# Chunk recurrence: the part of y that needs no u stacked into the u0 product, the rest accumulated in eight products of one shape

## The chip, the cores and the metric

The kernel runs on one core of one Trainium2 chip. The metric is device time in microseconds, the median of several runs. The engines of a core are TensorE (PE in the rows; its weight loads stand apart as PEld), VectorE (DVE), ScalarE (ACT), GpSimd (POOL) and SyncE (SP, which here issues most transfers). Each takes its instructions in a fixed order and waits at one until what that one needs is there.

## The reference

One layer of a hybrid encoder, 1024 tokens by 1024 columns in float32: an input projection, three token mixers side by side, an output projection with a residual, and a SwiGLU feed-forward part with a residual. The mixers are RWKV-7 time mixing (8 heads of 64), latent attention (4 heads) and stick-breaking attention (4 heads). The change is in the first. Its core is a recurrence over tokens, for each head with a 64x64 state S:

```
sa = S a_t
S  = S * w_t + sa b_t^T + v_t k_t^T
y_t = S r_t
```

After it, y is normed over each head, gets a bonus term, is multiplied by a gate and goes into the output projection.

## The kernel before, in words

The tokens are cut into 16 chunks of 64 (`NCH`, `L`). Inside a chunk the recurrence is solved by matrix products; only the state S goes from chunk to chunk. An early stage (`s1`, `s2`, `s3`) makes for each chunk and head the scaled vectors a and r (tile `AR`: a in the first 64 columns, r in the last), b and k (tile `BK`), and their masked products `gs` = (b|k) x (a|r), and writes them to the scratch tensor `d_ch` in DRAM. `d_lt` and `d_rx` are two parts of it. Another stage writes the inverse of I - A to the lower 64 rows of `d_rx`.

The recurrence itself is `chain_step(c)` (lines 1114 to 1155), called for the 16 chunks in turn. `chain_loads` brings 1 MB of `d_ch` into tile `CT` (its parts: `Lt`, `BKt`, `RX`) and v into the lower half of tile `SU`; both tiles have two buffers, and the transfers are issued from ACT's queue. `SU[:, 0]` is S stacked over v, `SU[:, 1]` is u stacked over v. Each step has four groups of products, eight heads each:

- u0 (L1124): `Lt[:, h, 0:64]` with S over v, 128 rows and 64 columns of weights. ACT copies the result (L1126, tile `u0s`).
- u (L1135): the inverse in `RX[64:128]` with u0, 64 rows and 64 columns. ACT copies it into `SU` (L1136).
- s (L1141): `BKt` with u over v, 128 x 64; DVE adds the decayed old state (tile `PS`) and writes the next S.
- y: for each head two products into the same place, one of `Lt[:, h, 64:128]` with u over v (L1148, 128 x 64) and one of `RX[0:64]` with S (L1149, 64 x 64).

A product in float32 is carried out as two instructions, so that eight products are 16 instructions in the rows. y of two chunks fills the upper and lower half of one bank of PSUM, and every second step `group_rows` copies it to SBUF and squares it (L1163 and L1165, ACT), and DVE sums the squares (L1168). After chunks 7 and 15 `rw_finish` norms and gates eight chunks at a time.

PSUM has eight banks in this stage: five under tag `b` for other work, one `av`, one `cu` (u0, u and s in turn) and one `cy` (y).

Between the groups `fill(us)` takes pieces of a background stream: first the last projections, then the two attentions, stick-breaking heads first (products z at L953 and L954, transposes wt at L890, products av at L908 to L915; scans C at L961 on DVE), latent heads after (products m at L976 to L978). A scheduler then sets each engine's order from the program's order and its own estimate; nothing moves on the chip after that. When the 16 steps are over, what is left of the stream runs by itself, and the output projection follows.

Of the kernel before, what the change touches and what calls it, by code (L numbers as in the profile page):

```python
# [20 lines left out]
P = 128  # L21
# [37 lines left out]
def trunk_kernel(ctx: ExitStack, tc: tile.TileContext, a: dict, out: bass.AP):  # L59
# [33 lines left out]
    # ---------------------------------------------------------------- constants  # L93
# [10 lines left out]
    # rotary tables  # L104
# [11 lines left out]
    # ---------------------------------------------------------------- DRAM scratch  # L116
# [19 lines left out]
    # ---------------------------------------------------------------- row norm and transpose  # L136
# [3 lines left out]
    def norm_transpose(pool, xt, dsts, tb):  # L140
        """rows of xt -> rms norm * gB -> transposed, split into dsts[h|l][group]"""
# [30 lines left out]
    # ---------------------------------------------------------------- streamed weights  # L172
# [27 lines left out]
    # xT[half][0 = h, 1 = l][group of 4 d blocks]  # L200
# [14 lines left out]
    def inproj_cols(c0, name):  # L215
        """w_in[:, c0:c0+128] as [c, t], one bank for each half of t"""
        if name in begun:
            return begun.pop(name)
        w = in_weights(c0, name)
        return [in_half(w, hf, name) for hf in range(2)]  # L220

    with tc.tile_pool(name="p0", bufs=2, reuse_waits="tile") as p0:
# [26 lines left out]
        for tb in range(NT):  # L249
# [3 lines left out]
            # the first projections, a quarter of t at a time  # L253
# [6 lines left out]
    # small constants of the attentions  # L260
# [11 lines left out]
    def shifted(dst, os_, cb):  # L272
        """dst[hf] = (1 - mu) p + mu p one step earlier"""
# [19 lines left out]
    # k_rope and the stick-breaking v, by row  # L293
# [25 lines left out]
    def sb_half(dst, blk, nm, hf, o):  # L319
        """[c, t] of two heads -> high and low parts, by head"""  # L320
# [11 lines left out]
    # ---------------------------------------------------------------- RWKV: projections, chunk products  # L332
    with tc.tile_pool(name="qa", bufs=1) as qa:
# [6 lines left out]
        # mask of the chunk products: rows (b|k) x s, columns (a|r) x t  # L340
# [14 lines left out]
        # up-projections of the two low ranks: K = 128 of (h, l) or (l, h), against the same rows twice  # L355
# [52 lines left out]
        def sigmoid3(dst, o, bias, t_):  # L408
            """dst = sigmoid(o - bias) = exp(-ln(1 + exp(bias - o)))"""
# [4 lines left out]
        def s1(pr, hf):  # L414
# [4 lines left out]
            # log decay / -kappa = sigmoid(w0 + u); its running sum in each chunk  # L419
# [16 lines left out]
        def s2(pr, hf):  # L436
# [20 lines left out]
            for e in range(2):  # L457
                cs_, rows_ = slice(hf * 8, hf * 8 + 8), slice(e * 64, e * 64 + 64)
                nc.sync.dma_start(d_lt[cs_, 0:64, 2 * pr + e, 0:64].rearrange("c k t -> k c t"), AR[rows_, :, 0, :])
                nc.sync.dma_start(d_rx[cs_, 0:64, 2 * pr + e, :].rearrange("c k t -> k c t"), AR[rows_, :, 1, :])  # L460
            tmp[n] = (AR, BK, av)

        def s3(pr, hf):
# [3 lines left out]
            # products of each chunk  # L467
            for q in range(2):
                c0 = hf * 8 + q * 4
                for e in range(2):  # L470
# [8 lines left out]
                    nc.sync.dma_start(d_lt[c0 : c0 + 4, 0:64, 2 * pr + e, 64:128].rearrange("c s t -> s c t"), gs[0:64, :, 64:128])  # L479
                    nc.sync.dma_start(d_a[2 * pr + e, c0 : c0 + 4].rearrange("c s t -> s c t"), gs[0:64, :, 0:64])  # L480
            # b, k times the decay of the whole chunk, transposed
            BKv = BK.rearrange("p c a t -> p c (a t)")
            tt(nc.vector, BKv, BKv, plt[:, pr, hf * 8 : hf * 8 + 8][:, :, None].to_broadcast([P, 8, 2 * L]), ALU.mult)
            # values, each head less its mean, by row
# [6 lines left out]
            # bonus * v  # L491
# [61 lines left out]
    # ---------------------------------------------------------------- two streams of work: the recurrence, and what fills its waits  # L553
# [4 lines left out]
    def fill(us):  # L558
        """trace about this much tensor-engine time of the background stream"""
# [29 lines left out]
    # ---------------------------------------------------------------- inverse of I - A_ab in every chunk; the other projections  # L589
# [28 lines left out]
    def inverse_steps(j0, j1):  # L618
        """back substitution of both diagonal blocks: XB[b] = (I - A_bb)^-T, one row for each step; GpSimd keeps the rows
        that are needed last up to date"""  # L620
# [24 lines left out]
    # four heads side by side on the partitions  # L645
# [10 lines left out]
    def merge_a(h):  # L656
        """(A_21 X_11) for the 16 chunks of a head, rows of the second half on partitions"""
# [14 lines left out]
    # MLA weights  # L672
# [936 lines left out]
```

## Time and profile before

| | |
|---|---|
| median of 3 runs | 1508.38 us |
| the three runs | 1508.38, 1509.59, 1500.39 us |
| span of the profiled execution, first to last instruction | 1507.6 us |
| its own time as a run | not given apart from the span |
| PE busy in the span | 1431.6 us (95%) |
| DVE busy | 918.1 us (61%) |
| ACT busy | 651.1 us (43%) |
| first u0 product to last y product | 434.6 to 723.7 us |

Only a span is known of the profiled execution, so sums are made against 1507.6 us; the median of the runs lies 0.8 us above it. A row of a product names weights as rows*columns and then the moving operand, as in `128*64 128x64`. PE's rows overlap: products are pipelined, and the time that a group takes on PE is best read from its start to the start of the next group. [...]

### The profile page before, as it was taken

The page shows a single profiled execution, that of the slowest core. Times are in us where ns is not written, and L with a number is a line of the kernel's source. Part 1 is how long each engine was busy: PE and PEld are TensorE (multiplying, and loading weights), DVE is VectorE, ACT ScalarE, POOL GpSimd, SP SyncE. Part 2 cuts the span into 40 slices and gives each one's busy share as a digit, 9 for nine tenths or more (in the row PEclk, how much of TensorE's full clock was granted, in tenths as well). Part 3 has the DMA queues.
Part 4 walks back from the last instruction along what each step waited for, and adds up shares of the span by engine and source line. Part 5 has one row for each costly group of instructions (what it writes and reads, how often), then busy time and mean ns, then how long its engine had stood idle before and what let it go on. Part 6 is the DMA issues. An engine that isn't in the chain of part 4 may idle for free.

```text
span 1507.6 us, 21884 instructions
## 1 busy us (share of the span) xinstructions
PE 1431.6 (95%) x7973; PEld 1164.0 (77%) x7973; DVE 918.1 (61%) x1308; ACT 651.1 (43%) x1256; POOL 639.4 (42%) x617
## 2 busy tenths in 40 slices
PE   7899999987979997999999899999999999999998
PEld 7677778876867876788788678888888888878786
DVE  5675566293336779654615885555555554798756
ACT  5745434223436656665723533233332332434342
POOL 1321111383233233212431676666665564645443
PEclk9999999998869998998999999999999999999999
DMA  7244656846558632542254153222222214953331
GB/s 210 64 112 117 153 122 164 178 113 155 144 167 247 187 116 88 153 135 85 92 174 160 39 186 105 98 93 90 88 100 101 102 50 183 379 175 114 98 133 70
DMA packets 222788, 201.31 MB, mean 134 GB/s; under 512 B 83373, under 2 KB 171738, under 8 KB 220762
## 3 DMA queue, kind: packets, MB, share of 16 engines
q1 hardware_dynamic: 212010, 175.28, 38.9%
q10 hardware_dynamic: 10672, 24.64, 5.0%
q8 instruction: 63, 1.03, 0.3%
q14 instruction: 43, 0.35, 0.1%
HBM read 131.95 MB, written 67.93 MB: 133 GB/s over the span
## 4 chain that ended last, share of the span: by engine, by line
PE 80%; DVE 11%; DMA 4%; ACT 2%; issue 2%; SPq 1%; POOL 0%; DVEq 0%; ACTq 0%; POOLq 0%
PE fd L197 4%; PE fd L198 4%; PE fd L196 4%; PE y L1149 2%; PE y L1148 2%; PE wt L890 2%; PE wo L198 2%; PE wo L197 2%; PE wo L196 2%; DVE XB L91 1%; PE u L1124 1%; PE s L1141 1%; PE u L1135 1%; PE ip_v L196 1%; DVE TM L91 1%
## 5 line engine op out<-in xcount | busy, mean ns | idle before, releaser
L91 POOL TENSOR_TENSOR l_h<-hr,h_h 128x512 fp32r<-128x512 f32 x77 | 106.9, 1389 | 105.5 <-ACT h_h L1270 101.7
L197 PE MATMUL fd<-l_w,h_h 128*128 128x512 f32 x308 | 119.7, 393 | 7.3 <-DVE l_w L91 7.3
L198 PE MATMUL fd<-h_w,l_h 128*128 128x512 f32 x308 | 118.5, 390 | 0.0
L91 DVE TENSOR_TENSOR l_w<-wd,h_w 128x512 fp32r<-128x512 f32 x77 | 89.7, 1174 | 47.0 <-ACT h_w L1270 47.0
L1270 ACT ACTIVATE h_h<-hr 128x512 fp32r<-128x512 f32 x77 | 48.7, 632 | 133.5 <-PE fd L197 89.2
L196 PE MATMUL fd<-h_w,h_h 128*128 128x512 f32 x308 | 83.6, 390 | 0.0
L91 POOL TENSOR_TENSOR l_ffn_w_up<-rffn_w_up,h_ffn_w_up 128x512 fp32r<-128x512 f32 x33 | 44.6, 1351 | 72.7 <-ACT h_ffn_w_up L1270 72.7
L197 PEld LDWEIGHTS fd<-l_w,h_h 128*128 128x128 f32 x308 | 57.8, 188 | 22.4 <-DVE l_w L91 10.6
L91 DVE TENSOR_TENSOR wtl<-wt,wth 128x512 fp32r<-128x512 f32 (+2 forms) x112 | 54.0, 492 | 34.5 <-PE av L914 12.0
L196 PEld LDWEIGHTS fd<-h_w,h_h 128*128 128x128 f32 x308 | 57.9, 188 | 12.1
L198 PEld LDWEIGHTS fd<-h_w,l_h 128*128 128x128 f32 x308 | 57.9, 188 | 11.8
L91 POOL TENSOR_TENSOR hid<-hid,up 128x512 f32<-128x512 f32 x44 | 62.7, 1425 | 9.6 <-DVE up L91 9.6
L91 POOL TENSOR_TENSOR l_ffn_w_gate<-rffn_w_gate,h_ffn_w_gate 128x512 fp32r<-128x512 f32 x33 | 47.5, 1442 | 28.0 <-ACT h_ffn_w_gate L1270 28.0
L895 ACT ACTIVATE wth<-wt 128x512 fp32r<-128x512 f32 (+2 forms) x112 | 48.9, 446 | 23.1 <-PE wt L890 10.7
L1449 ACT ACTIVATE hid<-hid 128x512 f32<-128x512 f32 x44 | 27.8, 634 | 57.2 <-DVE hid L91 57.2
L196 PE MATMUL wo<-woh,mix 128*128 128x512 f32 x128 | 50.5, 397 | 0.0
L198 PE MATMUL wo<-woh,mix 128*128 128x512 f32 x128 | 50.2, 394 | 0.0
L197 PE MATMUL wo<-wol,mix 128*128 128x512 f32 x128 | 50.1, 394 | 0.0
L1270 ACT ACTIVATE h_w<-wd 128x512 fp32r<-128x512 f32 x77 | 47.6, 618 | 0.9 <-PE fd L198 0.4
L1270 ACT ACTIVATE h_ffn_w_gate<-rffn_w_gate 128x512 fp32r<-128x512 f32 x33 | 20.7, 630 | 57.9 <-PE P4up L197 22.3
L1149 PE MATMUL y<-SU,CT 64*64 64x64 f32 x256 | 43.8, 254 | 0.0
L1148 PE MATMUL y<-SU,CT 128*64 128x64 f32 x256 | 43.4, 253 | 0.0
(565 smaller groups left out, 4503.9 us busy)
## 6 DMA issues: line engine op xcount, KB each, us to landing
CT<-d_ch ACTq DMA_DIRECT2D x15, 1024.0 KB
hr<-d_h SPq DMA_DIRECT2D x14, 1024.0 KB
rffn_w_gate<-in_ffn_w_gate_dram SPq DMA_DIRECT2D x11, 1024.0 KB
rffn_w_up<-in_ffn_w_up_dram SPq DMA_DIRECT2D x11, 1024.0 KB
d_h<-up SPq DMA_DIRECT2D x44, 256.0 KB
d_h<-hid SPq DMA_DIRECT2D x33, 256.0 KB
wd<-in_ffn_w_down_dram SPq DMA_DIRECT2D x8, 1024.0 KB
hr<-d_h SPq DMA_DIRECT2D x7, 768.0 KB
```

What stands on the lines that cost most here:

```text
L91: eng.tensor_tensor(o, x, y, op=op)
L196: nc.tensor.matmul(o, lh, rh, start=first, stop=False)
L197: nc.tensor.matmul(o, lh, rl, start=False, stop=False)
L198: nc.tensor.matmul(o, ll, rh, start=False, stop=last)
L890: nc.tensor.transpose(o[:, (sb * 2 + i) * P : (sb * 2 + i + 1) * P], W[i][:, (2 * g + sb) * P : (2 * g + sb + 1) * P], ident)
L895: nc.scalar.activation(wh[:, lo:hi], o[:, lo:hi], AF.Copy)
L1124: nc.tensor.matmul(o[0:64, hs[h]], Lt[:, h, 0:64], S[:, hs[h]], start=True, stop=True)
L1135: nc.tensor.matmul(o[0:64, hs[h]], RX[64:128, h, :], u0[:, hs[h]], start=True, stop=True)
L1148: nc.tensor.matmul(y[r0 : r0 + 64, hs[h]], Lt[:, h, 64:128], U[:, hs[h]], start=True, stop=False)
L1149: nc.tensor.matmul(y[r0 : r0 + 64, hs[h]], RX[0:64, h, :], S[0:64, hs[h]], start=False, stop=True)
L1270: nc.scalar.activation(hv, src, AF.Copy)
L1449: nc.scalar.activation(hid[f][hf], hid[f][hf], AF.Silu)
```

## The change

y is taken apart in another way. For each head, the r-part of `AR` and the (k,r)-products of `gs` now stand in the right 64 columns of `Lt`, below each other, so that one product of all 128 columns of `Lt` with S over v gives u0 in the upper 64 rows of a bank and the part of y that needs no u in the lower 64. `RX[0:64]` now holds the (b,r)-products, and eight products of it with u (64 x 64) are added onto that lower half. The bank is of tag `cy`, a new one for each chunk; u and s stay in `cu`. `y_rows` replaces `group_rows`: it copies y out after each step, 64 rows at a time, and squares and sums every second step, now from the copy in SBUF. In `s2` two transfers of halves of `AR` become one of the whole; in `s3` one transfer goes to `d_rx` instead of `d_lt`. The rest of the diff takes out comments.

```diff
@@ s2
-                nc.sync.dma_start(d_lt[cs_, 0:64, 2 * pr + e, 0:64].rearrange("c k t -> k c t"), AR[rows_, :, 0, :])
-                nc.sync.dma_start(d_rx[cs_, 0:64, 2 * pr + e, :].rearrange("c k t -> k c t"), AR[rows_, :, 1, :])
+                nc.sync.dma_start(d_lt[cs_, 0:64, 2 * pr + e, :].rearrange("c k t -> k c t"),
+                                  AR[rows_].rearrange("p c a t -> p c (a t)"))
@@ s3
-                    nc.sync.dma_start(d_lt[c0 : c0 + 4, 0:64, 2 * pr + e, 64:128].rearrange("c s t -> s c t"), gs[0:64, :, 64:128])
+                    nc.sync.dma_start(d_rx[c0 : c0 + 4, 0:64, 2 * pr + e, :].rearrange("c s t -> s c t"), gs[0:64, :, 64:128])
@@ chain_step
-        o = bank(f"u0_{c}", "cu")
+        yo = bank(f"y_{c}", "cy")
         for h in range(RWH):
-            nc.tensor.matmul(o[0:64, hs[h]], Lt[:, h, 0:64], S[:, hs[h]], start=True, stop=True)
+            nc.tensor.matmul(yo[:, hs[h]], Lt[:, h, :], S[:, hs[h]], start=h == 0, stop=True, skip_group_check=True)
         u0 = qr.tile([P, RWW], F32, tag="u0", bufs=1, name=f"u0s{c}")[64:128]
-        nc.scalar.activation(u0, o[0:64, :], AF.Copy)
+        nc.scalar.activation(u0, yo[0:64, :], AF.Copy)
...
-        if c % 2 == 0:
-            state["y"] = bank(f"y_{c}", "cy")
-        y = state["y"]
-        r0 = (c % 2) * 64
         for h in range(RWH):
-            nc.tensor.matmul(y[r0 : r0 + 64, hs[h]], Lt[:, h, 64:128], U[:, hs[h]], start=True, stop=False)
-            nc.tensor.matmul(y[r0 : r0 + 64, hs[h]], RX[0:64, h, :], S[0:64, hs[h]], start=False, stop=True)
+            nc.tensor.matmul(yo[64:128, hs[h]], RX[0:64, h, :], U[0:64, hs[h]], start=False, stop=True, skip_group_check=True)
         state["n"] = nxt
-        if c % 2 == 1:
-            group_rows(c // 2, y)
-            if c % 8 == 7:
-                side.append(rw_finish(c // 8, list(yn4), gnv["v"]))
+        y_rows(c, yo[64:128, :])
+        if c % 8 == 7:
+            side.append(rw_finish(c // 8, list(yn4), gnv["v"]))
         fill(FILL)
...
-    def group_rows(tb, y):
-        while side:
+    def y_rows(c, y):
+        while side and c % 2 == 0:
             fill(0.1)
-        yn = qr.tile([P, RWW], F32, tag="yn", bufs=4, name=f"yn{tb}")
-        nc.scalar.activation(yn, y, AF.Copy)
+        tb = c // 2
+        if c % 2 == 0:
+            yn4[tb % 4] = qr.tile([P, RWW], F32, tag="yn", bufs=4, name=f"yn{tb}")
+        yn = yn4[tb % 4]
+        nc.scalar.activation(yn[c % 2 * 64 : c % 2 * 64 + 64], y, AF.Copy)
+        if c % 2 == 0:
+            return
         sq = qr.tile([P, HALF], F32, tag="gq", bufs=1, name=f"gnq{tb}")
-        nc.scalar.activation(sq, y, AF.Square)
+        nc.scalar.activation(sq, yn, AF.Square)
...
-        yn4[tb % 4] = yn
```

The order on PE around the end of chunk 14, before (a row is one product here; s is the state, y the two kinds in turn, av and wt are background work, u_15 is u0 of the last chunk):

```order
L1141 MATMUL s_7021<-SU_6706,CT_6705 64x64 x8
L1148 MATMUL y_7031<-SU_6706,CT_6705 64x64
L1149 MATMUL y_7031<-SU_6706,CT_6705 64x64
L1148 MATMUL y_7031<-SU_6706,CT_6705 64x64
L1149 MATMUL y_7031<-SU_6706,CT_6705 64x64
...
L908 MATMUL av_1_7077<-wth_11_7015,vt_6790 128x256
...
L915 MATMUL av_1_7077<-wtl_10_7054,vt_6790 128x256
L1124 MATMUL u_15_7089<-SU_6908,CT_6907 64x64 x8
L890 MATMUL wt_22_7122<-ident,mw_4_6992 128x128
```

and the same place in the changed kernel (y_6768 is y of chunk 14, y_6954 the bank of chunk 15):

```order
L1142 MATMUL s_6893<-SU_6587,CT_6586 64x64 x8
L1145 MATMUL y_6768<-SU_6587,CT_6586 64x64 x8
L976 MATMUL m_4_512_6974<-mqk_6665,mqk_6663 128x128
...
L908 MATMUL av_1_6942<-wth_11_6887,vt_6671 128x256
...
L915 MATMUL av_1_6942<-wtl_10_6919,vt_6671 128x256
L890 MATMUL wt_22_6987<-ident,mw_4_6864 128x128
L1125 MATMUL y_6954<-SU_6780,CT_6779 128x64 x8
L890 MATMUL wt_21_6997<-ident,mw_4_6864 128x128
```

Where 16 products of two shapes stood in turn, eight of one shape stand; the u0 products write 128 rows, and other work stands between y and the next u0 as before. Over the whole recurrence PE's list changes the shape of its weights (rows*columns) 377 times before and 98 times now; whole blocks alone, with other work only between them, would make 335 and 78 of these. The one place where nothing stands between y and the next u0 is the end of chunk 1:

```order
L956 MATMUL z_2_0_4180<-sb_mask,identb 128x128
L1142 MATMUL s_4385<-SU_4080,CT_4079 64x64 x8
L1145 MATMUL y_4247<-SU_4080,CT_4079 64x64 x8
L1125 MATMUL y_4465<-SU_4259,CT_4258 128x64 x8
L890 MATMUL wt_00_4191<-ident,w_0_4137 128x128
```

There the u0 products moved up to y's end. Of the other steps the shortest distance is seven products.

On ACT, the order from the copy of y of chunk 3 to the copy of u0 of chunk 4, in the changed kernel (SU and CT are the next loads, yt a load for `rw_finish`, st, w and wth background work):

```order
L1162 ACTIVATE yn_4596<-y_4640 64x512
L1107 DMA SU_4867<-d_v 64x2x512
L1109 DMA CT_4866<-d_ch 128x2048
L957 ACTIVATE st_0_4507<-z_0_0_4511 128x128
L895 ACTIVATE wth_33_4523<-wt_33_4519 128x256
L1166 ACTIVATE gnq_4809<-yn_4596 128x512
...
L895 ACTIVATE wth_33_4523<-wt_33_4519 128x128
L1127 ACTIVATE u0s_4864<-y_4855 64x512
```

The copy of y stands ahead of the loads here as it did before, but now in every step instead of every second, and with 64 rows.

## Rows read from the trace of the kernel before

**Rows 1.** The page: busy time and share of each engine; who ends last, by engine.
```profile
PE 1431.6 (95%) x7973; PEld 1164.0 (77%) x7973; DVE 918.1 (61%) x1308; ACT 651.1 (43%) x1256; POOL 639.4 (42%) x617
...
PE 80%; DVE 11%; DMA 4%; ACT 2%; issue 2%; SPq 1%; POOL 0%; DVEq 0%; ACTq 0%; POOLq 0%
```

**Rows 2.** Chain of waits, 434 to 725 us: its shares by line.
```profile
by line: PE y L1149 12.0%; PE y L1148 11.3%; PE wt L890 10.7%; PE u L1124 7.1%; PE s L1141 5.6%; PE u L1135 5.5%; PE av L915 4.2%; PE z L953 3.7%; PE av L914 3.7%; DMA d_mk<-tqk 3.7%; PE m L976 3.2%; PE z L954 2.8%; PE m L977 2.6%; DVE C L9
```

**Rows 3.** Windows: length, busy us (instructions) per engine, granted clock, DMA share, GB/s.
```profile
434.00:460.00 26.00, 23.45 (x135) 19.13 (x136) 7.29 (x12) 8.44 (x16) 8.29 (x18) 0.58 0.71 234
460.00:570.00 110.00, 110.00 (x897) 87.73 (x895) 81.92 (x130) 68.92 (x163) 31.80 (x53) 0.92 0.60 177
570.00:620.00 50.00, 41.29 (x257) 33.91 (x256) 44.83 (x96) 31.75 (x78) 19.92 (x21) 0.86 0.24 75
620.00:725.00 105.00, 103.53 (x863) 86.41 (x862) 52.77 (x148) 59.66 (x153) 21.13 (x22) 0.90 0.40 122
```

**Rows 4.** Timeline of PE around a y block: start, us, line, tile, shape.
```profile
675.93 1.15 PE L1141 MATMUL s<-SU,CT 128*64 128x64 f32 x16
676.91 0.28 PE L1148 MATMUL y<-SU,CT 128*64 128x64 f32 x2
677.12 0.33 PE L1149 MATMUL y<-SU,CT 64*64 64x64 f32 x2
677.38 0.33 PE L1148 MATMUL y<-SU,CT 128*64 128x64 f32 x2
...
680.97 0.58 PE L915 MATMUL av<-wtl,vt 128*128 128x256 f32 x1
```

**Rows 5.** Timeline of PE: u block at 474 us and u0 block at 640 us, with what follows.
```profile
474.22 1.14 PE L1135 MATMUL u<-u0s,CT 64*64 64x64 f32 x16
475.30 0.50 PE L953 MATMUL z<-sqk,sqk 128*128 128x512 f32 x1
...
639.87 1.20 PE L1124 MATMUL u<-SU,CT 128*64 128x64 f32 x16
640.99 0.33 PE L890 MATMUL wt<-ident,mw 128*128 128x128 f32 x1
```

**Rows 6.** Timeline of PE: blocks whose weights have 128 columns, with what follows.
```profile
89.42 2.82 PE L474 MATMUL g<-AR,BK 64*128 64x128 f32 x32
92.17 1.16 PE L487 MATMUL vt<-cent,V 128*128 128x128 f32 x8
93.17 1.02 PE L493 MATMUL bo<-av,onesblk 128*128 128x512 f32 x2
...
398.81 0.95 PE L711 MATMUL lrkv<-bias_n,ctsckv 128*128 128x1 f32 x8
399.62 0.48 PE L196 MATMUL ukv<-ukvh,ct0ckv 128*128 128x512 f32 x1
```

**Rows 7.** Timeline of PE: half of the first y block, at the low clock.
```profile
444.01 0.42 PE L1148 MATMUL y<-SU,CT 128*64 128x64 f32 x2
444.36 0.47 PE L1149 MATMUL y<-SU,CT 64*64 64x64 f32 x2
...
447.19 1.94 PE L742 MATMUL tqk<-ident,Kt 128*96 128x128 f32 x8
```

**Rows 8.** Windows of PE alone: length, busy (instructions), granted clock, DMA share, GB/s.
```profile
632.00:634.00 2.00, 2.00 (x22) 1.00 0.20 74
634.00:636.00 2.00, 2.00 (x18) 1.00 0.00 0
636.00:638.00 2.00, 2.00 (x11) 0.65 0.15 40
638.00:640.00 2.00, 2.00 (x9) 0.50 0.86 292
640.00:642.00 2.00, 2.00 (x25) 1.00 0.98 373
...
588.00:590.00 2.00, 0.68 (x3) 0.50 0.32 82
```

**Rows 9.** Copies of u0 (L1126) and y (L1163) on ACT: ns, starts; what L1163 waited for.
```profile
L1126 ACT ACTIVATE u0s<-u x16: 588/589/592, 437.8 to 713.2; 64x512 f32<-64x512 f32 x16
...
L1163 ACT ACTIVATE yn<-y x8: 597/597/598, 469.4 to 723.9; 128x512 f32<-128x512 f32 x8
...
  PE y L1149: 18.0, 7
```

**Rows 10.** Weight loads and products of u (L1135): ns min/median/max, first and last start.
```profile
L1135 PEld LDWEIGHTS u<-u0s,CT x256: 129/135/224, 438.5 to 716.4; 64*64 64x64 f32 x128
L1135 PE MATMUL u<-u0s,CT x256: 217/218/364, 438.5 to 716.5; 64*64 64x64 f32 x128
```

**Rows 11.** Waits of PE in 434 to 725 us: total, times, longest.
```profile
PE u L1124 <- DMA CT<-d_ch: 6.1, 1, 6.1
...
PE u L1135 <- ACT u0s L1126: 1.9, 1, 1.9
```

**Rows 12.** Transfers of AR on SP's queue: ns of an issue.
```profile
L460 SPq DMA_DIRECT2D d_ch<-AR x16: 580/607/697, 65.7 to 245.4; - x16
```

## Prediction, made before the changed kernel was run

> **What bounds the kernel now.** I read the page first. PE is busy 95% of the span and ends 80% of the chain of waits [rows 1], so work taken off PE is the first thing that can shorten the run; DVE, with 61%, is the next. The change touches the stretch from 434 to 725 us. There the chain by line [rows 2] puts the two y lines on top: 12.0% and 11.3% of 291 us, 68 us. Next to them stand the background transposes; the DVE and DMA lines are small. The windows [rows 3] split the stretch in four. In the second (stick-breaking heads, y of chunks 1 to 7) PE has no gap in 110 us and DVE is at 74%. In the third (y of chunk 8 only) DVE is at 90% and PE at 83%: there PE waits for DVE. In the fourth (latent heads, chunks 9 to 15) PE is at 99%, DVE at 50%, ACT at 57%. PE's own list of waits names hardly anything [rows 11].
>
> The timeline shows why y is dear. At 676.91 us [rows 4] its 32 instructions run to 680.97 us: 4.06 us. Each pair of one shape starts 0.255 us after the pair of the other. The u block, 16 instructions of one shape, takes 1.08 us, 0.0675 each [rows 5]; a pair at that pace is 0.135 us, so a change of shape costs 0.12 us. y pays it 15 times in a block.
>
> **The change, part by part** (per block at the full clock, times 16).
>
> The y products. 32 instructions of two shapes become 16 of 64*64, the shape and count of the u block: 4.06 - 1.08 = 2.98 us less, 47.7 us in all. [...] Between s (128*64) and the new y there is a change of shape that was not there before: 16 x 0.12 = 1.9 us more.
>
> [...] The u blocks [rows 10] show loads of 135 ns and products of 218 ns, which in turn would need 353 ns per instruction; in the block one starts every 67.5 ns, on one group of rows and with float32 weights. [...]
>
> The u0 products. The weights go from 128 to all 128 columns of 128 rows; before, the block took 1.12 us [rows 5]. No row has 128*128 weights in float32 with 64 moving columns. Bounds [rows 6]: `g` (64*128, 128 moving columns) takes 2.75 us for 32, 1.4 for 16; `lrkv` (128*128, one column) 0.81 for 8, 1.6 for 16; `vt` (128*128, 128 columns) 1.00 for 8, 2.0 for 16. I take 1.8, between the two with the same weights: 0.68 x 16 = 10.9 us more, ends 4 and 14. On the other side u0 now has the shape of the background around it, so that one change of shape at its start goes: -1.9.
>
> Blocks cut by other work. The lists on PE hold 42 changes of shape beyond whole blocks before and 20 after, 22 x 0.12 = 2.6 us less.
>
> The clock. [...] A pass through 2 us windows puts it behind y blocks: the one at 632 to 636 us leaves 0.65 and 0.50 with PE busy all the time [rows 8]. [...]
>
> Sum on PE: -47.7 - 1.5 + 1.9 + 10.9 - 1.9 - 2.6 - 9 = -50 us.
>
> What does not reach the end. In the second stretch seven sixteenths of the terms without the clock (41 us), plus 4 of the clock's 9, are 22 us: PE would do it in 88 us, with DVE's 81.9 us in it at 93%. The highest share DVE has where it sets the pace is 90% [rows 3], 91 us, and there PE has gaps; I take 95 us, 7 us given back. The third stretch is DVE's already: its one block, 2.6 us, is given back whole. In the first stretch PE waits 6.1 us for the loads [rows 11] and other work goes on at the low clock: 1 us back. In the fourth, 23 us less would leave ACT at 73% and DVE at 64%: 2 us back. Together 12.6.
>
> ACT copies y 16 times instead of 8. A copy takes 0.6 us with 128 rows and with 64 [rows 9], so 4.8 us more. ACT has 40% of its time free, and it lost 18.0 us waiting for y's end in seven of the eight copies [rows 9], a wait that gets shorter with the block: 0, ends -4 and +5. The square now reads SBUF: nothing. DVE and POOL get nothing new. DMA: 32 transfers of `AR` become 16; at 0.6 us of issue on SP's queue [rows 12] that is 10 us less queue in 200 us, hidden behind PE: 0, ends -3 and 0. The loads of `CT` stand on ACT behind y's copy as before and leave earlier, with the block.
>
> Sum: -50 + 12.6 = -37.4 us. Against the span of 1507.6 us that is 1470.2; the median stands 0.8 us above the span, so **1471 us**. With the ends of u0 (-7, +3), the clock (-10, +9), what is given back (-6, +8) this case runs from 1450 to 1490.
>
> **The rivals.**
>
> *DVE keeps the second half.* PE's gain in the stick-breaking heads turns into waits for DVE, and the gaps bring the clock down as at 588 us, where 0.68 us busy of 2.00 goes with 0.50 [rows 8]. For it: DVE at 74% and then 90% [rows 3]. Against it: part of DVE's idle time there is waiting for PE. Then only the fourth stretch pays, some 18 us, and the first 3: 1487 us, 1480 to 1498. 14%.
>
> *The one bank for y (slower).* u0 of the next chunk needs the bank that ACT must first empty. ACT takes its work in order; if the copy stands behind background work, PE, in order too, stands still with all that is queued behind u0: background, u, s. The rows price one such pass through ACT in the open at 1.9 us [rows 11]. The gain is used up from 37/15 = 2.5 us per step; at two passes, 3.8 us, the loss is 57 - 37 = 20 us: 1528. For it: at the end of chunk 1 the u0 products follow y at once, and ACT copies every step. Against it: seven products or more stand between in the other steps, and ACT was ready before y's end in seven of eight [rows 9]. 4%.
>
> *Weight loads and products in turn.* If the new y ran its loads and products one after the other, 353 ns each pair [rows 10], a block would take 5.6 us, 16 x (5.6 - 4.06) = 25 us more than before for y alone, u0 on top: 1540 or later. The u block, which does not run so, is against it: 1%. [...]
>
> *It doesn't do what it says*: the y rows are long only as modelled, and the scheduler's new order loses elsewhere what it gains; 1500 to 1510. Against it: starts are not modelled, and the block's 4.06 us is taken from starts. 5%.
>
> **How the numbers follow.** The forecast has 76%; about 8 of these lie outside its own 1450 to 1490, evenly. To hold 80% I take 1450 to 1492, which adds part of the DVE case. Runs of this kernel spread over 9 us, 0.6%, so that about 1% (15 us) is what a measurement can tell from no change. Faster by over 1% (below 1493): nearly all of the forecast and most of the DVE case, 0.86. Within 1%: the rest of those two and the last rival, 0.09. Slower: the bank and the loads in turn, 0.05.
>
> **What would show it.** The new y blocks (L1145) should take 1.0 to 1.2 us for 16 instructions at the full clock, the u0 blocks (L1125) 1.4 to 2.0. First u0 to last y, 289 us before, should be about 252. The granted clock in the two long stretches should be 0.94 or more; if it is 0.90 again, that term was wrong. DVE should stand near 86% in the stick-breaking heads. PE waits for ACT at L1125 of over 1 us in more than two or three steps would show the bank's rival. If the y blocks are short and the time hasn't moved, PE did not set the end of this stretch, and the chain would show DVE or ACT lines where y stood.

## The result, and the profile after

The changed kernel takes 1468.72 us, median of 4 runs (1465.37 to 1469.48), against 1507.76 us for the kernel before, median of 4 runs (1500.39 to 1509.59). The ratio is 0.9756, with an interval of [0.9728, 0.9784]. The forecast was 1471 us, with a range of 1450 to 1492. The profiled run took 1469.48 us and its span is 1467.5 us.

The page of the changed kernel, busy time and share by engine, then the engines of the chain of waits; this answers to [rows 1].

```profile
PE 1384.8 (94%) x7717; PEld 1137.0 (77%) x7717; DVE 914.9 (62%) x1308; ACT 655.2 (45%) x1264; POOL 644.8 (44%) x617
...
PE 77%; DVE 10%; ACT 4%; DMA 4%; issue 3%; SPq 2%; POOL 1%; ACTq 0%; DVEq 0%; POOLq 0%
```

PE lost 46.8 us of busy time and 256 instructions, which are 128 products, and the run lost 39 us. DVE and POOL have the work that they had, ACT eight copies more.

The chain of waits of the changed kernel in its recurrence, 434 to 686 us, by line [rows 2].

```profile
by line: DVE C L961 6.6%; PE wt L890 6.1%; PE u L1136 6.0%; PE y L1125 5.6%; PE s L1142 5.4%; DVE w L91 5.2%; issue 5.1%; DMA d_mv<-mvhl 4.9%; PE y L1145 4.8%; DMA vt<-d_sv 4.3%; DVE wtl L91 3.4%; PE av L915 3.1%; PE av L914 2.9%; PE m L976
```

Before, two y lines stood on top with 23.3% of 291 us, 68 us, and u0 had 7.1%, 21 us. Now y (L1145) and u0 (L1125) together have 10.4% of 252 us, 26 us. A load that was not in the first rows, `vt`, has 4.3%, and DVE's scan comes first.

The timeline of PE in the changed kernel, around s and y of one chunk and u0 of the next (start, us, line, tile, shape); this answers to [rows 4] and to the u0 block of [rows 5].

```profile
655.55 1.15 PE L1142 MATMUL s<-SU,CT 128*64 128x64 f32 x16
656.63 1.14 PE L1145 MATMUL y<-SU,CT 64*64 64x64 f32 x16
657.70 0.87 PE L890 MATMUL wt<-ident,mw 128*128 128x128 f32 x6
...
672.00 1.90 PE L1125 MATMUL y<-SU,CT 128*128 128x64 f32 x16
```

From start to next start y takes 1.07 us (4.06 before). The u0 blocks take 1.70 to 1.76 us where nothing cuts them (1.12 before). From the first u0 to the last y it is 245 us, 289 before, 252 foretold.

Where the time came from is read best between four marks of the program: the first u0 product, the first stick-breaking score (`z`), the first latent score (`m`) and the first output product (`wo`). First the windows of the kernel before between these marks, then those of the changed kernel (the columns are those of [rows 3]; the granted clock is a share of full speed).

```profile
434.60:458.50 23.90, 21.95 (x120) 17.80 (x121) 6.86 (x11) 7.68 (x13) 7.70 (x18) 0.56 0.68 223
458.50:589.30 130.80, 123.43 (x970) 97.83 (x968) 101.38 (x165) 82.37 (x196) 43.46 (x66) 0.91 0.57 170
589.30:748.75 159.45, 153.50 (x1183) 127.33 (x1184) 99.10 (x267) 99.08 (x239) 40.18 (x39) 0.92 0.33 103
```

```profile
436.05:455.30 19.25, 15.90 (x102) 13.92 (x103) 5.32 (x8) 5.86 (x11) 8.57 (x16) 0.70 0.75 237
455.30:580.60 125.30, 110.10 (x874) 92.66 (x873) 108.69 (x171) 86.42 (x201) 47.25 (x69) 0.89 0.62 180
580.60:704.90 124.30, 119.74 (x1046) 105.23 (x1044) 91.89 (x263) 99.39 (x242) 37.24 (x37) 1.00 0.44 138
```

The stretch from the first u0 to the first score got 4.7 us shorter, the stick-breaking half 5.5 us, the latent half 35.2 us. In the stick-breaking half PE's busy time fell by 13.3 us, and its idle time rose from 7.4 to 15.2 us. In the latent half its busy time fell by 33.8 us, and the clock is 1.00 in place of 0.92: all 12.8 us that the clock had cost there (0.08 of 159.45) came back. Ahead of the first mark the changed run is 1.5 us later, behind the last one 3.8 us longer. All this compares one execution of each kernel, and the one of the kernel before ran at a low clock for its kind (0.961; 0.957 to 0.975 in the runs beside the experiments), so a few us of each difference are noise.

Three rows of the waits of the changed kernel, 434 to 682 us (total, times, longest).

```profile
ACT yn L1162 <- PE y L1145: 13.3, 7, 5.0
...
PE av L908 <- DMA vt<-d_sv: 2.6, 1, 2.6
...
PE y L1125 <- ACT yn L1162: 1.3, 2, 1.1
```

ACT still waits for y more than y's bank waits for ACT (third row: 1.3 us in two u0 blocks, 1.1 of it in one). The second row is small, but the chain passes that load from 463.61 to 474.37 us, and windows of 6 us show what it does to PE (length, then busy us of PE first, then the other engines; the granted clock follows POOL's column):

```profile
462.00:468.00 6.00, 4.92 (x35) 4.29 (x34) 5.35 (x8) 5.68 (x13) 3.32 (x5) 0.72 1.02 267
468.00:474.00 6.00, 3.90 (x23) 2.83 (x22) 4.10 (x6) 4.46 (x11) 1.19 (x2) 0.50 1.05 319
474.00:480.00 6.00, 5.49 (x40) 4.98 (x40) 2.67 (x5) 0.86 (x3) 1.25 (x3) 0.50 0.75 236
```

PE is idle 3.2 us of the first 12 and then runs at 0.50.

### The profile page after: what moved, and what is told of

It is laid out like the page before. It is cut to its first block, busy times and chain, and to the rows that moved or that the text cites. A ratio compares the mean times of both kernels' runs of the same rounds, so it can differ in the third digit from the quotient of the medians.

```text
span 1467.5 us, 21365 instructions
## 1 busy us (share of the span) xinstructions
PE 1384.8 (94%) x7717; PEld 1137.0 (77%) x7717; DVE 914.9 (62%) x1308; ACT 655.2 (45%) x1264; POOL 644.8 (44%) x617
## 4 chain that ended last, share of the span: by engine, by line
PE 77%; DVE 10%; ACT 4%; DMA 4%; issue 3%; SPq 2%; POOL 1%; ACTq 0%; DVEq 0%; POOLq 0%
PE fd L197 4%; PE fd L198 4%; PE fd L196 4%; PE wo L197 2%; PE wo L198 2%; PE wo L196 2%; DVE C L961 1%; PE ip_v L196 1%; PE wt L890 1%; PE u L1136 1%; PE ip_r L198 1%; PE ip_v L197 1%; PE ip_r L196 1%; PE ip_v L198 1%; PE ip_r L197 1%
## 5 line engine op out<-in xcount | busy, mean ns | idle before, releaser
L1270 ACT ACTIVATE h_h<-hr 128x512 fp32r<-128x512 f32 x77 | 48.7, 632 | 134.1 <-PE fd L197 88.9
L895 ACT ACTIVATE wth<-wt 128x512 fp32r<-128x512 f32 (+2 forms) x112 | 47.4, 446 | 12.5 <-DVE wtl L91 6.5
L91 DVE TENSOR_TENSOR up<-hid,hid 128x512 f32<-128x512 f32 x22 | 28.2, 1322 | 19.6 <-POOL hid L91 19.6
L91 DVE TENSOR_TENSOR wd<-wd,wd 128x512 f32<-128x512 f32 x44 | 39.7, 933 | 0.6
```

Source lines behind the costliest of these rows:

```text
L91: eng.tensor_tensor(o, x, y, op=op)
L895: nc.scalar.activation(wh[:, lo:hi], o[:, lo:hi], AF.Copy)
L1270: nc.scalar.activation(hv, src, AF.Copy)
```

## The experiments

Each was timed against the kernel before on its own chip, so ratios are compared, not microseconds. "Clock loss" is (1 - mean granted clock) x span, a mean over a kernel's runs, without the longest run of a2 (1524.96 us) and of a3 (1545.67 us). "Changes" are changes of the weights' shape between neighbours on PE, in the program's order, from the first u0 to the last y; weights of 96 rows, those of the latent scores, count here as 128 (as a shape of their own they make 448 changes before and 164 in the change, by the rows of the two traces).

| kernel | changes | ratio to before | interval | clock loss, us |
|---|---|---|---|---|
| before | 377 | 1 | | 51 to 54 |
| the change, again (b0) | 98 | 0.9728 | 0.9706 to 0.9749 | 40 |
| a1: y regrouped | 166 | 0.9735 | 0.9683 to 0.9787 | 35 |
| e: one shape, in turn | 147 | 0.9712 | 0.9660 to 0.9765 | 33 |
| c1: grouped, other places | 165 | 0.9703 | 0.9679 to 0.9727 | 34 |
| a2: u0 widened only | 335 | 0.9996 | 0.9963 to 1.0028 | 40 |
| a3: change, s and y in turn | 291 | 1.0087 | 1.0052 to 1.0122 | 72 |

**a1, the order alone.** The kernel before, its sixteen y products in two groups of eight:

```diff
-            nc.tensor.matmul(y[...], Lt[:, h, 64:128], U[:, hs[h]], start=True, stop=False)
+            nc.tensor.matmul(y[...], Lt[:, h, 64:128], U[:, hs[h]], start=h == 0, stop=False, ...)
+        for h in range(RWH):
             nc.tensor.matmul(y[...], RX[0:64, h, :], S[0:64, hs[h]], start=False, stop=True, ...)
```

> The kernel before, with one edit: the sixteen y products of a chunk stand in two groups, first the eight of 128*64 weights, then the eight of 64*64, where they took turns. Number of products, weights, banks and transfers are those of before. Theory of the change of shape (0.12 us at each on TensorE): the y block has one change of shape inside instead of 15, so it goes from 4.06 us to 2.2 to 2.4 us; 16 blocks give 26 to 30 us on TensorE, and the granted clock rises behind them as it did with the change, 5 to 9 us. With what DVE keeps in the stick-breaking half, the kernel is 20 to 32 us faster than before. Theory of the count (the gain of the change came from 256 fewer instructions): y blocks stay near 4.06 us and the time within 3 us of before.

1461.8 us, ratio 0.9735. The timeline of PE in a1:

```profile
659.06 1.15 PE L1141 MATMUL s<-SU,CT 128*64 128x64 f32 x16
660.04 1.10 PE L1148 MATMUL y<-SU,CT 128*64 128x64 f32 x16
661.07 1.14 PE L1150 MATMUL y<-SU,CT 64*64 64x64 f32 x16
662.14 0.39 PE L908 MATMUL av<-wth,vt 128*128 128x256 f32 x1
```

The 32 instructions take 2.10 us in place of 4.06. The whole gain of the change is there with all 256 products of y kept and nothing stacked, 40 us, more than the 20 to 32 expected: the clock loss fell by 16 us where 5 to 9 were put down. The theory of the count falls.

**e, shape apart from everything else that alternates.** The kernel before, the second product of each pair over 128 rows (it adds a term to y that doesn't belong there; what is timed is the same):

```diff
-            nc.tensor.matmul(y[...], RX[0:64, h, :], S[0:64, hs[h]], start=False, stop=True)
+            nc.tensor.matmul(y[...], RX[:, h, :], S[:, hs[h]], start=False, stop=True)
```

> The kernel before, with one edit: the second y product of each pair takes all 128 rows of its weights and of S (a wrong y: the lower rows add a product that does not belong there). The 32 y instructions of a chunk still take turns between the same two weights and accumulate in the same pairs, but all have 128*64 weights. It parts the shape from everything else that alternates (operands, pairs of accumulation). Theory of the change of shape: the y block takes 2.15 us in place of 4.06, 377 changes of shape in the stretch become 147, 230 x 0.12 = 28 us less on TensorE, and with some of the clock the kernel is 25 to 40 us faster than before. Rival, taking turns itself costs (operands, accumulation in pairs): the block stays near 4.06 us, the time within 3 us of before.

1462.46 us, ratio 0.9712, a gain of 43 us. The first and the last of the 16 pieces of one y block of e, and what follows:

```profile
643.49 0.28 PE L1148 MATMUL y<-SU,CT 128*64 128x64 f32 x2
643.60 0.28 PE L1149 MATMUL y<-SU,CT 128*64 128x64 f32 x2
...
645.12 0.28 PE L1148 MATMUL y<-SU,CT 128*64 128x64 f32 x2
645.24 0.28 PE L1149 MATMUL y<-SU,CT 128*64 128x64 f32 x2
645.45 0.39 PE L915 MATMUL av<-wtl,vt 128*128 128x256 f32 x1
```

Pairs follow each other after 0.117 us here and after 0.255 us where the shapes differ [rows 4]. The turns, the accumulation in pairs, the banks and the number of products are the same; the second product has 128 rows in place of 64, and that is its shape. So 0.14 us is the price of one change of shape.

**a2, the widening alone.** The kernel before, u0 with 128 columns of weights, the upper half unread:

```diff
-            nc.tensor.matmul(o[0:64, hs[h]], Lt[:, h, 0:64], S[:, hs[h]], start=True, stop=True)
+            nc.tensor.matmul(o[:, hs[h]], Lt[:, h, :], S[:, hs[h]], start=True, stop=True)
```

> The kernel before, with one edit: the u0 products take all 128 columns of weights and write 128 rows, the upper 64 of which nobody reads; y is left as it was. This prices the widening alone. Theory: the u0 block goes from 1.12 to 1.7 to 1.8 us (1.70 to 1.76 us measured in the changed kernel), 16 x 0.6 = 10 us more on TensorE, less 2 to 4 us for the changes of shape that go at its start and end, since the work around it has 128*128 weights: the kernel is 3 to 10 us slower than before. Rival, the columns cost nothing and the block's 1.7 us in the changed kernel comes from its place: the block stays near 1.12 us and the kernel is 0 to 4 us faster.

1502.89 us, ratio 0.9996: between 6 us faster and 4 us slower, so of the expected 3 to 10 us only the lower end is possible. The block did get longer, as a timeline row of a2 with its follower shows:

```profile
688.02 1.90 PE L1124 MATMUL u<-SU,CT 128*128 128x64 f32 x16
689.76 0.83 PE L890 MATMUL wt<-ident,mw 128*128 128x128 f32 x6
```

1.74 us, 0.62 more, 10 us in all. Against it stand 42 changes of shape fewer (5 to 6 us) and a clock loss 10 us smaller. The rival, that the columns are free, is wrong as well.

**a3, the shapes put back in turn.** The changed kernel, its s and y products interleaved:

```diff
                 nc.tensor.matmul(o[0:64, hs[h]], BKt[:, hs[h]], U[:, hs[h]], ...)
-            tt(nc.vector, nxt[1][0:64, 0, :], o[0:64, :], PS, ALU.add)
-        for h in range(RWH):
-            nc.tensor.matmul(yo[64:128, hs[h]], RX[0:64, h, :], U[0:64, hs[h]], ...)
+                nc.tensor.matmul(yo[64:128, hs[h]], RX[0:64, h, :], U[0:64, hs[h]], ...)
+            tt(nc.vector, nxt[1][0:64, 0, :], o[0:64, :], PS, ALU.add)
```

> The changed kernel, with one edit: the eight s products (128*64 weights) and the eight y products (64*64) of a chunk take turns; the same 32 instructions with the same operands, in another order. Theory of the change of shape: the two blocks take 2.14 us together at full clock now, and 4.06 us in turn, as the 32 instructions of the y block of the kernel before did; 15 chunks give 29 us more on TensorE; the granted clock behind these blocks falls again, in the latent half too, where it is 1.00 now, 5 to 10 us more; the stick-breaking half, where TensorE waits for DVE some 10 us, takes up a part. Together 22 to 40 us slower than the changed kernel, so near the time of the kernel before. Theory of the count: the same instructions take the same time, 0 to 3 us slower, for the later S alone.

1514.57 us, ratio 1.0087, 50 us and more above the change's 0.9756 or 0.9728, where 40 was the upper end. First two rows of its timeline and the follower of the last, then its windows between the marks `z`, `m` and `wo`:

```profile
652.08 0.33 PE L1142 MATMUL s<-SU,CT 128*64 128x64 f32 x2
652.34 0.33 PE L1143 MATMUL y<-SU,CT 64*64 64x64 f32 x2
...
656.19 0.77 PE L890 MATMUL wt<-ident,mw 128*128 128x128 f32 x5
```

```profile
456.08:602.10 146.02, 137.57 (x854) 112.07 (x854) 102.47 (x167) 84.30 (x196) 41.98 (x65) 0.77 0.50 144
602.10:745.96 143.86, 136.81 (x1061) 115.36 (x1059) 97.84 (x266) 101.69 (x246) 39.92 (x42) 0.98 0.40 122
```

The 32 instructions take 4.11 us (2.15 in the change), 29 us over 15 chunks, as expected. The clock adds a loss of 72 us in place of 40; the two make 61 us, so some 10 of them are taken up elsewhere. The low clock stands where it was not expected: 0.77 in the stick-breaking half, and 0.98 in the latent half, where the theory wanted it low.

**a4, d1 and d2: does DVE hold the stick-breaking half?** a4 gives the products of block 7 to GpSimd; d1 (the change) and d2 (before) cut DVE's products short:

```diff
-    SB_POOL, MLA_POOL = (1, 3, 5), (1, 3, 5)
+    SB_POOL, MLA_POOL = (1, 3, 5, 7), (1, 3, 5)
```

```diff
-            tt(nc.gpsimd if i in SB_POOL else nc.vector, w[:, k0:k1], w[:, k0:k1], C[:, k0 + 1 : k1 + 1], ALU.mult)
+            kx = k1 if i in SB_POOL else k0 + 32
+            tt(nc.gpsimd if i in SB_POOL else nc.vector, w[:, k0:kx], w[:, k0:kx], C[:, k0 + 1 : kx + 1], ALU.mult)
```

> The changed kernel, with one edit: the products of weights and running product of query block 7 (two of 128x512 per head of the stick-breaking attention, 0.75 us each on DVE) go to GpSimd, as those of blocks 1, 3 and 5 do. Theory that DVE sets the pace of the stick-breaking half of the recurrence (57.1 us busy of 60 in 490 to 550, 27.1 of 28 in 550 to 578, while TensorE is idle 10.6 us): DVE loses 4 x 1.5 = 6 us of work, GpSimd has it free (24 of 60 busy) and takes some 17 us more; the first scores of the latent half come 3 to 6 us earlier, and the kernel is 2 to 6 us faster than the changed one. Rival, TensorE's order and not DVE's load sets the pace (the transposes that follow need GpSimd's result, which comes 2.5 to 3 us later): 0 to 6 us slower.

> The changed kernel, with one edit: in the stick-breaking attention DVE multiplies only 32 of up to 512 columns of a block's weights by the running product (the rest stays unmultiplied, a part of the computation left out); the waits stay. This takes some 20 us of DVE's work out of the first half of the recurrence and nothing else. Theory that DVE sets the pace there and took back a part of the gain: TensorE is idle 15.2 of the 125.3 us from the first stick-breaking scores to the first latent ones; 6 us of that are for loads; 6 to 11 us go, and the kernel is 5 to 11 us faster than the changed one. Rival, DVE's load does not matter (what moves TensorE's idle time is its own order and the loads): within 2 us of the changed kernel.

> The kernel before, with the same edit in the stick-breaking attention: DVE multiplies 32 of up to 512 columns, a part of the computation left out. Theory: before the change TensorE is idle only 7.4 of 130.8 us in that half, since its own longer work covers DVE; 2 to 5 us go, and the kernel is 2 to 5 us faster than before. So the gap between the two kernels without this work of DVE is 42 to 48 us, against 39 with it: the difference is what DVE took back. Rival: the same gain in both, the gap stays at 39 us.

a4: 1469.87 us, ratio 0.9766 [0.9700, 0.9832]. d1: 1465.42 us, 0.9735 [0.9686, 0.9784]. d2: 1498.72 us, 0.9969 [0.9935, 1.0003]. None can be told from its parent, and a4's interval (10 us either way) is too wide for the 2 to 6 us that were asked of it. The window from `z` to `m` of a4, then that of d1, then that of d2:

```profile
449.03:572.71 123.68, 108.31 (x875) 91.46 (x873) 102.41 (x165) 86.39 (x202) 52.74 (x75) 0.92 0.63 187
```

```profile
446.81:572.37 125.56, 114.47 (x874) 97.65 (x872) 96.19 (x171) 87.74 (x202) 41.36 (x68) 0.85 0.62 183
```

```profile
447.67:568.63 120.96, 120.04 (x966) 95.35 (x965) 89.06 (x157) 80.08 (x191) 36.00 (x61) 0.94 0.60 178
```

In d1 DVE has 12.5 us less work there and the half is as long as before the edit: PE's idle time fell from 15.2 to 11.1 us, and the clock took it back (0.85). In d2 the half is 9.8 us shorter than in the kernel before, and PE's idle time falls from 7.4 to 0.9 us: there PE did wait for DVE, as [rows 3] say, though the whole run hardly shows it. From d2 to d1 the ratio falls by 0.023, 35 us, give or take 9, against 0.024 to 0.027 with DVE's full work. The theory that DVE took back a part of the gain foretold 42 to 48 us and finds no support; a few us are not excluded.

**b1, the merged transfer cut in two again.**

```diff
-                nc.sync.dma_start(d_lt[cs_, 0:64, 2 * pr + e, :]..., AR[rows_]...)
+                nc.sync.dma_start(d_lt[cs_, 0:64, 2 * pr + e, 0:64]..., AR[rows_, :, 0, :])
+                nc.sync.dma_start(d_lt[cs_, 0:64, 2 * pr + e, 64:128]..., AR[rows_, :, 1, :])
```

> The changed kernel, with the store of the decayed a and r halves into the chunk loads' area cut in two transfers again, as before the change (16 more issues, 512-byte runs become 256-byte ones). Theory: these stores lie in the projections, where neither the queue nor the chain of waits ends on them: within 2 us of the changed kernel. Rival, part of the gain came from the merged transfer: 3 to 8 us slower than the changed kernel, with the first chunk load landing later.

1466.61 us, ratio 0.9737 [0.9686, 0.9788]: the transfers carry nothing.

**b0, f1, c1 and f2, side by side on one chip.** b0 is the change. f1 gives the first head's values a tile whose memory is free early:

```diff
         head_load(0)
+        head_values(0)
         attend = bg_attend()
...
-            vt = values[H] = left["qc"].tile([P, NT, P], F32R, tag="vt", bufs=2, name=f"vt{H}")
+            vt = values[H] = (cp.tile([P, NT, P], F32R, tag="gB", name="vt0") if H == 0
+                              else left["qc"].tile([P, NT, P], F32R, tag="vt", bufs=2, name=f"vt{H}"))
```

c1 is the kernel before with y's two groups apart (f2 is c1 with f1's edit):

```diff
         nc.scalar.activation(U[0:64, :], o[0:64, :], AF.Copy)
+        for h in range(RWH):
+            nc.tensor.matmul(y[...], RX[0:64, h, :], S[0:64, hs[h]], start=h == 0, stop=False, ...)
...
         for h in range(RWH):
-            nc.tensor.matmul(y[...], Lt[:, h, 64:128], U[:, hs[h]], start=True, stop=False)
-            nc.tensor.matmul(y[...], RX[0:64, h, :], S[0:64, hs[h]], start=False, stop=True)
+            nc.tensor.matmul(y[...], Lt[:, h, 64:128], U[:, hs[h]], start=False, stop=True, ...)
```

> The changed kernel itself, unaltered, to stand beside the next three on one chip. Expected: the ratio to the kernel before measured first, 0.973 to 0.979, so about 1467 us against about 1504.

> The changed kernel, with one edit: the values of the first stick-breaking head (vt, 512 KB) get a tile of their own among the constants' memory, so that their load is issued before the recurrence and no longer at 463 us, behind the stores that free its memory. Theory of the loads: in the stick-breaking half of the changed kernel TensorE stands some 6 us for this load (465 to 475), and the granted clock is 0.50 from 467 to 481 behind that wait, up to 7 us more; both go, and the kernel is 5 to 13 us faster than the changed one. Rival, the stretch is held by the transfers as a whole (83% of the DMA engines' time in 434 to 490) or by DVE and GpSimd later in that half: within 3 us of the changed kernel.

> The kernel before, with the y products grouped by shape and put beside blocks of their own shape: the eight of 64*64 weights (RX and S) right behind u, the eight of 128*64 weights (Lt and U) right behind s; nothing stacked, all 256 products are kept. Theory that the shapes carry the gain and stacking adds little: TensorE has 165 changes of shape in place of 377 and 98, and 3.23 us of products per chunk (u0 and y) in place of 2.81, so 8 us of changes and 7 us of products more than the changed kernel; but the grouped kernel of the first call was 1461.8 us all the same, as TensorE waited and ran at the low clock less; c1 is within 6 us of the changed kernel and 33 to 45 us faster than before. Rival, stacking carries a part of its own: c1 is 8 to 15 us slower than the changed kernel.

> The kernel c1 (grouped, not stacked) with the early load of the first head's values. Theory of the loads: 4 to 13 us faster than c1, which has the same load at the same place of the program. Rival: within 3 us of c1. If both theories hold, one of f1 and f2 is faster than both the kernel before and the changed kernel, near 1455 us.

b0: 1466.04 us, ratio 0.9728, as expected.

f1: 1465.19 us, ratio 0.9731 [0.9708, 0.9754], no gain. Yet its theory held where it spoke. Windows from `z` to `m` and from `m` to `wo`, first of b0, then of f1, with the last stretch of f1 behind its last y:

```profile
450.85:577.74 126.89, 109.86 (x874) 92.77 (x873) 108.45 (x171) 86.47 (x201) 47.16 (x69) 0.89 0.61 176
577.74:702.06 124.32, 119.77 (x1046) 105.30 (x1044) 91.82 (x263) 99.40 (x242) 37.13 (x37) 1.00 0.44 138
```

```profile
446.32:559.50 113.18, 103.67 (x868) 87.51 (x866) 100.10 (x160) 86.03 (x201) 43.85 (x63) 0.95 0.69 198
559.50:702.72 143.22, 129.91 (x1060) 111.84 (x1060) 100.64 (x276) 101.14 (x245) 44.36 (x44) 0.94 0.38 119
...
684.00:703.00 19.00, 11.53 (x53) 7.75 (x52) 9.82 (x23) 6.20 (x11) 8.92 (x8) 0.73 0.00 1
```

The stick-breaking half is 13.7 us shorter: PE's idle time goes from 17.0 to 9.5 us and the clock from 0.89 to 0.95; PE's wait for `vt`, 4.4 us in b0, is gone. The marks part the work a little otherwise here: 8.3 us of DVE's work, about half of it from `rw_finish`, and 14 of PE's instructions stand ahead of `m` in b0 and behind it in f1. The second half gives 18.9 us back. In b0 the background ends after the chunks (last latent score 689.6 us, last y 677.3); in f1 it ends before them (671.2 and 684.0). Nothing is left to cover the end of the recurrence: in the last row above PE is idle 7.5 us of 19, at 0.73. The waits of PE in f1, 680 to 705 us, show for what:

```profile
PE yt L1205 <- POOL yn L91: 6.6, 4, 5.0
```

c1: 1460.14 us, ratio 0.9703, 5.9 us under b0 by the medians, with intervals that overlap. It is the fastest of all, but cannot be told from the change. The scheduler set its 64*64 group mostly behind u0, not behind u, so that it saved no change against a1. PE is busy 253.4 us from the first u0 to `wo` (246.8 in b0), as 3.23 us of products per chunk against 2.81 make it; its clock loss over the whole run, 34 us in place of 40, pays for that.

f2: 1474.29 us, ratio 0.9778 [0.9752, 0.9804], 14 us slower than c1. Both theories missed. Its two halves are 122.8 and 136.8 us long, against 118.9 and 132.1 of c1, and the longest wait of PE in them is one of 4.2 us for DVE in `wt`; I can't say which of the moved loads did it.

## Why the prediction was right, and where it was not

**Sum and sign.** 1468.72 us against 1471, a gain of 39.0 us against 37.4. The likeliest case came true, but in part by luck. Between the first u0 and `wo` PE's busy time fell by 53.1 us (50 foretold) and its idle time rose by 7.8, which makes 45.3; 5.2 us went outside that stretch (1.5 ahead, 3.8 behind), for which the sum had nothing. The clock gave back 6 us more than was put down, and these two cancelled.

**The y and u0 products.** Right: 1.07 us against 1.08, and 1.70 to 1.76 against 1.8. The mechanism, changes of shape, is shown from three sides (a1, a3, e). The price of a change was put at 0.12 us; e and [rows 4] give 0.14. What happens inside TensorE at a change is not shown. The rival of loads and products in turn, 5.6 us a block, is out: 16 instructions whose weights all stand in the same 64 rows take 1.07 us (656.63 to 657.70 us in the changed kernel). No run shows by itself the 1.5 us that the sum has beside the 47.7: the first block took 6.41 us before (444.01 to 447.19 us [rows 7] and 449.06 to 452.29, all at 0.50) and takes 1.21 us in the change (448.23 to 448.61 and 449.62 to 450.45, at 1.00). That is 5.20 us less, where 2.98 and 1.5 were put down.

**What the prediction did not see.** It credited the change with halving y and charged it for u0. The experiments part these: grouping alone (a1, c1, e) gives 0.9703 to 0.9735, grouping with stacking 0.9728 to 0.9756. Stacking adds nothing that these runs can tell; its products (0.42 us less per chunk) show on PE's busy time and not in the end.

**The clock.** Under-sized: 9 us, with ends 0 and 19. No run shows that term by itself; it was an estimate of mine, half of the 19 us that the clock costs in the second and fourth stretch of [rows 3] (0.08 of 110 us and 0.10 of 105 us). By the windows above the loss between the first u0 and `wo` is 35 us before and 20 in the changed profile; over the runs that stand beside b0 it is 54 and 40 us. The place was wrong, too: 4.7 us came back ahead of the first score, 12.8 in the latent half, and nothing in the stick-breaking half, where the clock stayed at 0.89 against the 0.94 of the prediction's own sign. The cause holds better than this looks, for the traces part two kinds of fall. First four us of the kernel before that end in a fall (they hold the y block of [rows 4]) and two us behind it, then the same of the changed kernel:

```profile
677.00:681.00 4.00, 4.00 (x35) 2.92 (x32) 0.82 (x3) 1.20 (x5) 2.05 (x2) 1.00 0.02 4
681.00:683.00 2.00, 2.00 (x13) 1.78 (x13) 0.72 (x2) 0.28 (x1) 0.00 (x0) 0.50 0.24 65
```

```profile
539.00:543.00 4.00, 2.23 (x19) 1.45 (x19) 3.89 (x6) 3.01 (x8) 3.28 (x3) 1.00 0.85 273
544.00:546.00 2.00, 2.00 (x10) 1.48 (x10) 2.00 (x4) 0.69 (x2) 0.10 (x1) 0.50 0.00 0
```

Between the first score and `wo` the clock of the kernel before falls nine times. Seven of these falls come like the first, with PE busy throughout and a block of two shapes in turn right ahead; the low stretches behind them add up to 37.5 us and cost about 19. Falls like that are also in the traces of d2 and a3, which keep two shapes in turn: within one block the pairs start every 0.26 us and then, from 457.6 us in d2 and from 518.3 us in a3, every 0.40 us, with no idle time of PE in or ahead of the block. They are in none of nine kernels without such blocks (the change, b0, b1, a1, c1, d1, e, f1, f2), where PE has been idle for 0.7 us or more in the 6 us ahead of each fall, as in the second pair of rows (1.77 us of 4). e is among the nine, so it is the two shapes and not the turns. That the y blocks bring these falls is thus borne out, in one execution of each kernel, and the whole of it came back, near the 19 us of the upper end; new falls behind PE's waits, 13.8 us of loss in the stick-breaking half, took some of it again. Why a block of two shapes does this while the rows show PE busy is not shown (the ends of PE's rows are modelled), nor why only some do: 16 such blocks make seven falls before, and a3 has 0.98 in its latent half. So the clock loss of a run does not go with the number of changes (a2: 335 and 40 us; b0: 98 and 40 us).

**What is given back.** The step that failed: "I take 95 us", because DVE sets the pace. The size was near (idle time of PE in the stick-breaking half rose by 7.8 us, where 9.6 were given back in the second and third stretch), DVE stands at 87% as foretold, and still DVE is not what held it: with 12.5 us less of its work the half is as long (d1). The score products on PE (z, 128 instructions in each kernel) show where the half lost. Their first 32 take 30.1 us before, 37.3 in the change, 37.8 in b0, 36.7 in d1, and 30.1 in f1, which moves the load of `vt` ahead. From there to the first latent score it is 100.7 us before, then 88.0, 89.1, 88.9 and 83.1. So the change gained 12.7 us in the later part and lost 7.2 in the first 32, where PE waits for that load and runs at 0.50 behind the wait. So most of what was given back lies there; f1 moves other loads on SP's queue as well, and that it was this one alone is read from the chain, not shown. DVE's 90% beside a waiting PE in [rows 3], true of the kernel before (d2), had misled me.

**The rest.** Zero for the merged transfer: right (b1). Zero for ACT's eight more copies: right, 13.3 us of waiting for y remain. The one bank of y: 1.3 us, so that rival is out. The shares by half were wrong: about 15 and 21 us foretold, 5.5 and 35.2 measured; that their sum came out is luck. For the stick-breaking half the rival in which DVE keeps it was nearer, with another cause.

**What stays open.** Why a block of two shapes pulls the clock down with PE busy, and why not each one; the 3.8 us behind the last mark in the changed kernel (4.0 in b0); why f2 is slow. Untried: f1 with less background per chunk, so that both streams end together.

## What to carry to other kernels

Before reducing a number of small products, look at the order of their weights' shapes: if the timeline shows pairs of two shapes in turn, group them first; here that took no product away and gave all of the gain (a1, 0.9735). When an engine at 87% stands beside a gap, take its work away in an experiment before calling it the bound; the chain of waits named the load that the shares did not. When two streams share an engine, a wait removed from one can let it run dry before the other ends, and the gain turns into a new wait there (f1: 13.7 us won in one half, 18.9 lost in the other).

## What the runs showed of the hardware

Weights of one shape let instructions follow each other every 0.058 us (128*64, e) to 0.067 us (64*64, the change), even in turn between two weights and in pairs of accumulation; a change between 128*64 and 64*64 costs 0.14 us at the full clock (0.255 against 0.117 us from pair to pair), and in the a3 block 15 such changes nearly double the time (2.15 to 4.11 us). Float32 weights of 128*128 with 64 moving columns take 0.106 to 0.11 us per instruction (1.70 to 1.76 us for 16, in the change and in a2). The granted clock fell from 1.00 to 0.50 with PE busy throughout only behind blocks of two shapes in turn: seven times in the kernel before, also in d2 and a3, and never in the nine kernels named above, which have no such blocks.
